# An MLP cut into eight equal chunks of seven products, an early modulation, a fourth place for weights, and smaller edits to mask and router bias

## The chip, the cores and the metric

The kernel runs on one core of a Trainium2 chip. The metric is the time of one execution on the device in microseconds (us); lower is better. The engines are TensorE (PE, matrix products), VectorE (DVE), ScalarE (ACT), GpSimd (POOL) and SyncE (SP, which issues nearly all transfers). Each engine runs its instructions in the order in which they were written to it.

## The reference

Two transformer blocks over 1024 rows of 1024 float32 numbers, one after the other. What the change touches:

```python
# first block: causal conv + retention mixer, cross attention to 256 memory rows, then
h = h + square(relu(rmsnorm(h, norm_mlp_w) @ up_w)) @ down_w      # up 1024x4096, down 4096x1024
x = rmsnorm(h, norm_f_w)
# second block
mod   = silu(c)     @ w_ada + b_ada                               # w_ada 1024x6144, six vectors of 1024
mod_c = silu(c_ctx) @ w_ada + b_ada                               # only its first two vectors are used
h = rmsnorm(x, g_mix) * (1 + sc1) + sh1
# q, k, v and a short convolution from h @ w_in; rope; 8 query heads on 2 key heads
# softmax over [sink, 256 context keys, latent keys with |i - j| <= 128]
x = x + gt1 * (concat(att, conv) @ w_out)
h2 = rmsnorm(x, g_ffn) * (1 + sc2) + sh2
# router: softmax(h2 @ w_router); each of 16 experts takes its 128 best rows; silu gate, up, down
x = x + gt2 * experts(h2);  return rmsnorm(x, g_final)
```

## The kernel before, in words

Every large product is made of float32r matmuls on split numbers: a number is a rounded part and a remainder, and a product is three matmuls (hi·hi, hi·lo, lo·hi; `mm3`). A matrix of weights arrives as a raw unit of 128x1024 float32 (`raw_unit`, 512 KB, issued by SP) and is split by ACT (a copy, L119) and DVE (a subtraction, L120) into a place `w`.

The program goes through its stages in this order: conv and retention; the mixer's output product (`add_out` on `w_out_tm`, tile `wo`); cross attention; the MLP; the second block's norm with keys and values (`kv`), queries, attention, output product, router, top rows, experts. A scheduler merges the stages' instructions on each engine from the order of the code and the priorities (`tc.high_priority`); what it decides is fixed when the kernel is built.

The MLP holds the normalised input of 512 rows as eight tiles for each half of the rows (`hm[0]`, `hm[1]`), and the sum of 1024 rows as eight tiles `acc`. It walks over nine chunks of the hidden dimension (in blocks of 128, `fb`): two chunks of two blocks, and seven of four. The first two and the last chunk are standard (`mlp_chunk`): "up" of each block and half, then "dn" by output tile, three matmuls for each block. The last is ordered by row tile, so that tile 0 of `acc` is complete first. The six between (`mlp_chunk_7`) replace the eight block products of a 2x2 block matrix product by seven, with sums and differences of blocks made on DVE: seven products of 24 matmuls (tiles `dnA`, `dnB`, `dnC`). The "up" results are squared into T places 4 to 7 as full numbers, and split into the operands `x..`/`s..`.

The modulation (`mod_blocks`) multiplies each of 48 units of `w_ada` (through the one place R32) with the rows `crow` (silu of c and c_ctx, T places 4 to 7) in reductions on DVE (L767): four for each of the first 16 units, two for the others. The table `MOD_BLOCKS` says after which chunk of the MLP how many units stand.

After the MLP each of the eight row tiles is normalised twice (L955 to L973; `z` is L972), with many one-column instructions (L169 to L180, L966 to L970) on DVE. Four `z` tiles are transposed (`ptT`), scaled on ACT (L234) and split on DVE (L235, L236) into `hT`, which the products `kv` read; `kT` (L1018) is the first transpose of a finished key tile.

PSUM banks go round in rings: `pm = Ring([0, 1, 2, 3, 4])` for products, `pt = Ring([5, 6, 7])` for transposes (`ptT`), `pu = Ring([4, 5, 6, 7])` for the "up" tiles of `mlp_chunk_7`. The input tiles `hin` from which `hm[1]` is made lie in R17 to R20, and `mlp_chunk_7` puts its first operands into R16 to R19.

Of the kernel before, what the change touches and what calls it, by code (L numbers as in the profile page):

```python
# [10 lines left out]
F32 = mybir.dt.float32  # L11
F32R = mybir.dt.float32r
# [8 lines left out]
MLP_CHUNKS = [2, 2] + [4] * 7  # L21
MOD_BLOCKS = [8, 8] + [5] * 6 + [2]
# [13 lines left out]
def tile_kernel(ctx: ExitStack, tc: tile.TileContext, d, out, stop=None, dbg=None):  # L36
# [93 lines left out]

    def wunits(src, i0, n, ahead=1500):

        res = []
        with tc.high_priority(offset=ahead):
            for u in range(i0, i0 + n):
                raw = raw_unit(src[u])
                w = sb.tile([128, 2, 1024], F32R, tag=f"W{w_ring[0]()}", bufs=1, name=nm("w"))
                split(w[:, 0, :], w[:, 1, :], raw)
                res.append(w)
        return res  # L140
# [531 lines left out]
    add_out(x_d, d["w_out_tm"], mT, range(8), h1_d, "h1", lambda: R(hxR(), [128, 512], name="hx"))  # L672
    hq[0] = normed(h1_d, 0, g_x, [19, 20, 21, 16], H[0], "hq")
# [75 lines left out]

    mod_d = dram([4, 1024], "mod_d")  # L750
    mws = T(8, [128, 512], name="mws")
    mjunk = mws[:, 0:256].bitcast(BF)
    mpart = mws[:, 256:384].rearrange("p (h n) -> p h n", h=2)
    crow = {}
    for o in range(2):
        for h in range(2):
            c = bcast(T(4 + 2 * o + h, [128, 512], name="crow"), d["c_rows"][o, h * 512:(h + 1) * 512], 512)
            act.activation(c, c, AF.Silu)
            crow[o, h] = c

    def mod_blocks(b0, n):

        for b in range(b0, b0 + n):
            raw = load(R(32, [128, 1024], name="wada"), d["w_ada"][b])
            for o in range(2 if b < 16 else 1):
                for h in range(2):
                    dve.tensor_tensor_reduce(out=mjunk, in0=raw[:, h * 512:(h + 1) * 512], in1=crow[o, h],  # L767
                                             op0=OP.mult, op1=OP.add, scale=1.0, scalar=0.0,
                                             accum_out=mpart[:, h, 48 * o + b:48 * o + b + 1])

    rr = Ring([0, 1])
    rv = Ring([2, 3])
    UT = {0: [16, 21, 22, 23], 1: [17, 18, 19, 20]}

    def mlp_chunk(ch, ch0, fbs, last):

        uT = {0: [], 1: []}
        for fb in range(fbs):
            uni = wunits(d["up_fm"], ch0 + fb, 1)
            for half in range(2):  # L780
                p = B(pm(), "up")
                fm_block(p, uni[0], half_of(hm, half))
                r = T(rr(), [128, 512], name="relu")
                act.activation(r, p, AF.Relu)
                v = T(rv(), [128, 512], name="sq")
                act.activation(v, r, AF.Square)
                ut = R(UT[half][fb], [128, 2, 512], F32R, name="uT")
                dve.tensor_copy(ut[:, 0, :], v)
                dve.tensor_sub(ut[:, 1, :], v, ut[:, 0, :].bitcast(F32))
                uT[half].append(ut)  # L790
        nu = fbs // 2
        if not last:
            order = [(nb, t) for nb in range(2) for t in range(8)]
        else:
            order = [(nb, t) for t in range(8) for nb in range(2)]
        uni = {}
        for nb, t in order:
            if nb not in uni:
                uni[nb] = wunits(d["down_tm"], ch0 + nb * nu, nu)
            sl = slice(nb * 512, (nb + 1) * 512)  # L800
            p = B(pm(), "dn")
# [756 lines left out]
```

## Time and profile before

| | |
|---|---|
| median of three runs | 2522.18 us (2521.58 to 2522.71) |
| the profiled execution's own time | 2525.16 us |
| its span in the trace | 2523.2 us (1.96 us less than its time) |
| PE busy over the span | 2400.3 us, 95% |
| DVE busy | 1898.4 us, 75% |
| ACT busy | 1240.8 us, 49% |
| mean granted clock of PE | 0.98 |

A share over the whole span says little here, since PE is the limit in most stages and waits in a few: the stages have to be read one by one. The busy time of pipelined matmuls overlaps; their spacing is what counts.

### The profile page before, as it was taken

What the parts mean: (1) busy time and instruction counts of PE and PEld (TensorE: products, weight loads), DVE (VectorE), ACT (ScalarE), POOL (GpSimd) and SP (SyncE); (2) the same over time, 40 slices, a digit from 0 to 9 for tenths busy, and PEclk for the clock granted to TensorE, in tenths of its full rate; (3) what the DMA queues carried; (4) which work ended last, traced back from release to release, by engine and by line L of the source; (5) the groups of instructions that cost most, each with busy time, mean ns of one, the idle gap of its engine ahead of it and who ended that gap; (6) DMA issues with size and microseconds to landing.
All of it is one profiled execution on the core that took longest, in us unless ns stands there. A gap on an engine that the chain in (4) does not pass through costs nothing. (4 is left out here: it accounts for less than half of the span.)

```text
span 2523.2 us, 31350 instructions
## 1 busy us (share of the span) xinstructions
PE 2400.3 (95%) x11327; PEld 1947.9 (77%) x11327; DVE 1898.4 (75%) x3269; ACT 1240.8 (49%) x1891; POOL 56.5 (2%) x37
## 2 busy tenths in 40 slices
PE   7999899999999999999999899999985999999995
PEld 6887677888878788888888777777873888888774
DVE  6999893554566877775566758776658999999887
ACT  6113552454451342334335725554334888887775
POOL 0000000000000000000000000000000110101100
PEclk9999999999999999999999999999996999999998
DMA  4233555425353244421222121114674999999994
GB/s 179 100 127 112 175 163 180 155 77 179 116 180 101 92 134 143 143 79 42 67 84 78 70 83 51 38 55 155 235 262 154 388 399 394 393 394 391 355 372 158
DMA packets 139051, 444.88 MB, mean 176 GB/s; under 512 B 15728, under 2 KB 20240, under 8 KB 138896
## 3 DMA queue, kind: packets, MB, share of 16 engines
q1 hardware_dynamic: 134144, 425.58, 47.6%
q0 software_dynamic: 4752, 17.30, 2.7%
q8 instruction: 89, 1.46, 0.2%
q14 instruction: 66, 0.54, 0.1%
HBM read 390.37 MB, written 52.45 MB: 176 GB/s over the span
## 5 line engine op out<-in xcount | busy, mean ns | idle before, releaser
L119 ACT ACTIVATE w<-raw 128x1024 fp32r<-128x1024 f32 x576 | 601.4, 1059 | 608.6 <-PE up L146 107.5
L120 DVE TENSOR_TENSOR w<-raw,w 128x1024 fp32r<-128x1024 f32 x576 | 692.6, 1223 | 164.8 <-ACT w L119 153.3
L144 PE MATMUL up<-hm,w 128*128 128x512 f32 x512 | 199.6, 390 | 0.0
L145 PE MATMUL up<-hm,w 128*128 128x512 f32 x512 | 199.4, 389 | 0.0
L146 PE MATMUL up<-hm,w 128*128 128x512 f32 x512 | 199.3, 389 | 0.0
L424 DVE SCALAR_TENSOR_TENSOR y<-u,small,y 128x1023 f32<-128x1023 f32 (+25 forms) x120 | 146.2, 1267 | 0.4
L767 DVE CUSTOM_DVE_ANT_0 mws<-wada,crow 128x512 bf16<-128x512 f32 x128 | 88.1, 688 | 49.0 <-DMA wada<-w_ada 47.3
L144 PEld LDWEIGHTS up<-hm,w 128*128 128x128 f32 x512 | 96.0, 188 | 20.3 <-DVE acc L846 0.3
L145 PEld LDWEIGHTS up<-hm,w 128*128 128x128 f32 x512 | 96.1, 188 | 19.8
L146 PEld LDWEIGHTS up<-hm,w 128*128 128x128 f32 x512 | 96.1, 188 | 19.8
L145 PE MATMUL dn<-w,x1T 128*128 128x512 f32 x256 | 101.5, 396 | 2.0 <-DVE w L120 2.0
L145 PE MATMUL ga<-w,x1T 128*128 128x512 f32 x256 | 101.7, 397 | 1.7 <-DVE w L120 1.7
L144 PE MATMUL dn<-w,x1T 128*128 128x512 f32 x256 | 102.3, 400 | 0.5 <-ACT w L119 0.5
L146 PE MATMUL ga<-w,x1T 128*128 128x512 f32 x256 | 101.2, 396 | 0.0
L146 PE MATMUL dn<-w,x1T 128*128 128x512 f32 x256 | 101.2, 395 | 0.0
L145 PE MATMUL up<-w,x1T 128*128 128x512 f32 x256 | 100.8, 394 | 0.2 <-DVE w L120 0.2
L144 PE MATMUL ga<-w,x1T 128*128 128x512 f32 x256 | 100.7, 393 | 0.0
L146 PE MATMUL up<-w,x1T 128*128 128x512 f32 x256 | 99.8, 390 | 0.0
L144 PE MATMUL up<-w,x1T 128*128 128x512 f32 x256 | 99.8, 390 | 0.0
L839 PE MATMUL dnB<-w,s 128*128 128x512 f32 x288 | 71.3, 403 | 5.8 <-ACT s L119 4.1
L846 DVE TENSOR_TENSOR acc<-dnA,acc 128x512 f32<-128x512 f32 x96 | 63.2, 686 | 11.4 <-PE dnA L839 10.9
L1353 POOL DMA_INDIRECT xs<-hf_d,IT x16 | 19.8, 1237 | 2264.9 <-DVE IT L1340 1925.6
(460 smaller groups left out, 5814.4 us busy)
## 6 DMA issues: line engine op xcount, KB each, us to landing
raw<-experts SPq DMA_DIRECT2D x384, 512.0 KB, 7.2
wada<-w_ada SPq DMA_DIRECT2D x48, 512.0 KB, 3.6
raw<-down_tm SPq DMA_DIRECT2D x38, 512.0 KB, 3.6
raw<-up_fm SPq DMA_DIRECT2D x32, 512.0 KB, 3.6
raw<-w_out_tm SPq DMA_DIRECT2D x24, 512.0 KB, 4.1
raw<-w_in_fm SPq DMA_DIRECT2D x20, 512.0 KB, 4.0
h_d<-hx SPq DMA_DIRECT2D x32, 256.0 KB, 2.9
raw<-xq_fm SPq DMA_DIRECT2D x16, 512.0 KB, 4.9
```

What stands on the lines that cost most here:

```text
L119: act.activation(hi, src, AF.Copy)
L120: dve.tensor_sub(lo, src, hi.bitcast(F32))
L144: pe.matmul(out_, l[0], r[0], start=first, stop=False)
L145: pe.matmul(out_, l[0], r[1], start=False, stop=False)
L146: pe.matmul(out_, l[1], r[0], start=False, stop=last)
L424: dve.scalar_tensor_tensor(yc[:, s:], uc[:, :1024 - s], convw[:, c, 30 - s:31 - s], yc[:, s:], op0=OP.mult, op1=OP.add)
L767: dve.tensor_tensor_reduce(out=mjunk, in0=raw[:, h * 512:(h + 1) * 512], in1=crow[o, h], op0=OP.mult, op1=OP.add, scale=1.0, scalar=0.0, a ...
L839: pe.matmul(bank[j], l, r, start=first and f + i == 0, stop=f == 1 and i == 2, skip_group_check=not first)
L846: dve.tensor_add(a[:, sl], bank[j], a[:, sl])
L1353: nc.gpsimd.indirect_dma_start(out=xs, out_offset=None, in_=hf_d, in_offset=bass.IndirectOffsetOnAxis(ap=IT[:, e:e + 1], axis=0))
```

## The change

The MLP has eight chunks of four blocks, all of seven products. The first takes the "up" tiles in another order (`first`), and the last its seven products in another order (`end`). A pair of registers R34 and R35 is a fourth place for split weights and R33 a fourth for raw units in the MLP; later R33 to R35 hold raw units of the experts. Room for them comes from a DMA scratch of 4096. The modulation is 64 blocks of two reductions with one pair of `crow` (T4, T5), so that 16 units are loaded twice. Of these blocks 28 stand right after the first `add_out`, with three places, the others in the MLP's chunks with one place. In attention the mask is added to the two outer blocks of 128 keys only, after the first part of the scores. The router's bias product `lb` is made right after the modulation. The diff, cut:

```diff
-MLP_CHUNKS = [2, 2] + [4] * 7
-MOD_BLOCKS = [8, 8] + [5] * 6 + [2]
+MLP_CHUNKS = 8
+MOD_EARLY = 28
+MOD_BLOCKS = [2, 6, 6, 6, 6, 6, 4, 0]
...
+    class Pair:
+        def __init__(self, i):
+            self.t = [R(i + j, [128, 1024], F32R, name="w") for j in range(2)]
+        def __getitem__(self, ix):
+            _, j, sl = ix
+            return self.t[j][:, sl]
+    def w_place():
+        i = w_ring[0]()
+        if i == "pair":
+            return Pair(34)
+        return sb.tile([128, 2, 1024], F32R, tag=f"W{i}", bufs=1, name=nm("w"))
...
     add_out(x_d, d["w_out_tm"], mT, range(8), h1_d, "h1", lambda: R(hxR(), [128, 512], name="hx"))
+    crow = []
+    wada = Ring([22, 23, 32])
+    def mod_blocks(b0, n):
+        for b in range(b0, b0 + n):
+            o, i = divmod(b, 48)
+            if i == 0 or b == MOD_EARLY:
+                crow[:] = [bcast(T(4 + h, [128, 512], name="crow"), d["c_rows"][o, h * 512:(h + 1) * 512], 512)
+                           for h in range(2)]
+                for c in crow:
+                    act.activation(c, c, AF.Silu)
+            raw = load(R(wada(), [128, 1024], name="wada"), d["w_ada"][i])
+            for h in range(2):
+                dve.tensor_tensor_reduce(out=mjunk, in0=raw[:, h * 512:(h + 1) * 512], in1=crow[h],
+                                         op0=OP.mult, op1=OP.add, scale=1.0, scalar=0.0,
+                                         accum_out=mpart[:, h, b:b + 1])
+    mod_blocks(0, MOD_EARLY)
+    wada = Ring([32])
...
-    def mlp_chunk_7(ch0):
+    def mlp_chunk(ch0, first, end):
...
-        for f in range(2):
+        for f, half in ((0, 0), (1, 0), (0, 1), (1, 1)) if first else ((0, 0), (0, 1), (1, 0), (1, 1)):
...
+        else:
+            ...
+            product(bB, xD, t1, True)
+            add(bB, 1, 1)
+            product(bA, xE, t2, False)
+            add(bA, 0, 1)
+            ...
+            product(bB, xG, w22, False)
+            add(bB, 0, 1)
+            bC = [B(4 + j, "dnC") for j in range(4)]
+            product(bC, xF, w21, True)
+            add(bC, 0, 0)
+            product(bA, xB, t3, False)
+            add(bA, 1, 1)
+            product(bA, xC, t4, False)
+            add(bA, 1, 0)
...
+    w_ring[0] = Ring([0, 1, 2, "pair"])
+    raw_ring[0] = Ring([("raw", 0), ("raw", 1), ("raw", 2), ("R", 33)])
+    mb = MOD_EARLY
+    for ch in range(MLP_CHUNKS):
+        mlp_chunk(4 * ch, ch == 0, ch == MLP_CHUNKS - 1)
...
-                    pe.matmul(pl, identr, wmr[:, m0:m0 + nl], start=True, stop=False)
-                    for l in range(2):
-                        pe.matmul(pl, qT[:, h, :], K2[2 * kv + l][:, lo * 128:lo * 128 + nl],
-                                  start=False, stop=(l == 1))
+                    pe.matmul(pl, qT[:, h, :], K2[2 * kv][:, lo * 128:lo * 128 + nl], start=True, stop=False)
+                    if nl == 384:
+                        pe.matmul(pl.rearrange("p (b n) -> p b n", b=3)[:, 0:3:2, :], identr,
+                                  wmr[:, 0:256].rearrange("p (b n) -> p b n", b=2), start=False, stop=False)
+                    else:
+                        o = 0 if t > 0 else 128
+                        pe.matmul(pl[:, o:o + 128], identr, wmr[:, o:o + 128], start=False, stop=False)
+                    pe.matmul(pl, qT[:, h, :], K2[2 * kv + 1][:, lo * 128:lo * 128 + nl], start=False, stop=True)
...
-                       + [("raw", i) for i in range(3)] + [("R", i) for i in H[1] + [32]])
+                       + [("raw", i) for i in range(3)] + [("R", i) for i in H[1] + [32, 33, 34, 35]])
...
-    nc = bacc.Bacc("TRN2", target_bir_lowering=False, num_devices=1)
+    nc = bacc.Bacc("TRN2", target_bir_lowering=False, num_devices=1, dynamic_dma_scratch_size=4096)
```

Where the MLP begins, PE before has the transposes of the first `hin` tile (row tile 4 of the second half), then "up" matmuls, and the transposes of the next tile after 15 of them:

```order
L146 MATMUL wo_5925<-w_5833,oT_5545 128x512
L247 MATMUL ptT_6020<-ident,hin_5952 128x128
L247 MATMUL ptT_6028<-ident,hin_5952 128x128
L247 MATMUL ptT_6036<-ident,hin_5952 128x128
L144 MATMUL up_6119<-hm_5621,w_6116 128x512
L145 MATMUL up_6119<-hm_5621,w_6116 128x512
```

PE in the changed kernel at the same place:

```order
L164 MATMUL wo_6045<-w_5953,oT_5665 128x512
L265 MATMUL ptT_6140<-ident,hin_6072 128x128
L265 MATMUL ptT_6148<-ident,hin_6072 128x128
L265 MATMUL ptT_6156<-ident,hin_6072 128x128
L265 MATMUL ptT_6140<-ident,hin_6089 128x128
L265 MATMUL ptT_6148<-ident,hin_6089 128x128
L265 MATMUL ptT_6156<-ident,hin_6089 128x128
L162 MATMUL up_6229<-hm_5741,w_6226 128x512
L163 MATMUL up_6229<-hm_5741,w_6226 128x512
```

The transposes of the second tile now stand ahead of every "up" matmul. Up to the last transpose of the fourth tile (32 transposes in all) there are 24 matmuls of `up_6229`, 3 of `up_6407` and 5 of `dnA`; the next 24 matmuls of the first half (`up_6264`) come behind it. Before, 76 matmuls of "up" and "dn" stand in that stretch.

DVE where the MLP ends, in the changed kernel: `acc_6204` to `acc_6210` are the row tiles of the first half, `acc_6212` to `acc_6218` those of the second; `dnC` completes the first half, `dnA_10282` to `dnA_10285` are the banks of the last product, and L191 is the reciprocal in the norm of row tile 0:

```order
L831 TENSOR_TENSOR acc_6204<-dnC_10590,acc_6204 128x512
...
L831 TENSOR_TENSOR acc_6212<-dnA_10282,acc_6212 128x512
L831 TENSOR_TENSOR acc_6214<-dnA_10283,acc_6214 128x512
L831 TENSOR_TENSOR acc_6216<-dnA_10284,acc_6216 128x512
L831 TENSOR_TENSOR acc_6218<-dnA_10285,acc_6218 128x512
L191 RECIPROCAL y_10719<-y_10717 128x1
L187 TENSOR_SCALAR y_10753<-y_10748 128x1
L979 TENSOR_TENSOR acc_6208<-acc_6208,bc_10678 128x1024
```

Before, five of the eight `z` stand ahead of DVE's last addition of a "dn" tile, and 73 instructions stand between that addition and the first instruction on a finished `kv` tile (L986). Now no `z` stands ahead of it, and 163 instructions stand between: 83 more of one column, five more `z`, four more products with the norm's gain (L962 before, L979 now), and two splits of weights fewer.

DVE ahead of the first `wo` product's operands in the changed kernel; `mT` are the operands, L710 the reductions of the modulation:

```order
L619 TENSOR_SCALAR z_2772<-yc_2751,y_2757,y_2770 128x512
L710 ISA mws_3797<-wada_3816,crow_3798 128x512
L710 ISA mws_3797 128x1
L710 ISA mws_3797<-wada_3816,crow_3800 128x512
...
L710 ISA mws_3797<-wada_3824,crow_3800 128x512
L710 ISA mws_3797 128x1
L122 TENSOR_TENSOR mT_2781<-zsl_2779,mT_2781 128x512
L122 TENSOR_TENSOR mT_2791<-zsl_2789,mT_2791 128x512
L710 ISA mws_3797<-wada_3828,crow_3798 128x512
```

Before, the splits of `mT` (L120) stand right behind the `z` (L601). Up to the last of the operands the reductions of about eleven blocks are now between them, and on SP seven loads of `w_ada` stand ahead of the loads of `yr`, from which half of the operands are made.

## Rows read from the trace of the kernel before

**Rows 1.** The page's first part: busy time, share of the span, instructions.
```profile
PE 2400.3 (95%) x11327; PEld 1947.9 (77%) x11327; DVE 1898.4 (75%) x3269; ACT 1240.8 (49%) x1891; POOL 56.5 (2%) x37
```

**Rows 2.** Windows: length, PE, PEld, DVE, ACT, POOL busy (instructions), clock, DMA share, GB/s.
```profile
363.40:396.00 32.60, 31.04 (x160) 23.77 (x161) 23.27 (x58) 18.57 (x30) 0.00 (x0) 1.00 0.51 168
396.00:461.00 65.00, 65.00 (x288) 53.83 (x288) 21.68 (x47) 13.07 (x19) 0.00 (x0) 1.00 0.59 190
705.80:733.40 27.60, 23.88 (x117) 18.22 (x115) 19.80 (x46) 20.24 (x31) 0.00 (x0) 1.00 0.56 194
...
850.00:900.00 50.00, 44.18 (x177) 34.50 (x176) 42.56 (x74) 18.16 (x27) 0.00 (x0) 0.93 0.41 127
...
1351.80:1389.80 38.00, 38.00 (x170) 31.40 (x169) 31.84 (x111) 24.87 (x47) 0.00 (x0) 1.00 0.18 70
1389.80:1411.30 21.50, 17.36 (x131) 15.18 (x128) 21.28 (x82) 17.24 (x33) 0.00 (x0) 1.00 0.42 148
...
2000.00:2300.00 300.00, 300.00 (x1384) 246.34 (x1384) 287.99 (x277) 244.29 (x260) 28.59 (x17) 1.00 1.03 394
```

**Rows 3.** Timeline of PE in a seven-product chunk: start, us, what, count.
```profile
1242.58 5.60 PE L839 MATMUL dnA<-w,x 128*128 128x512 f32 x24
1248.02 0.39 PE L144 MATMUL up<-hm,w 128*128 128x512 f32 x1
```

**Rows 4.** Timeline, first seven-product chunk; in brackets idle time ahead and its end.
```profile
849.27 0.69 DVE L767 CUSTOM_DVE_ANT_0 mws<-wada,crow 128x512 bf16<-128x512 f32 x1 [2.51 <-DMA wada<-w_ada]
...
851.48 0.60 ACT L821 ACTIVATE sq<-up 128x512 f32<-128x512 f32 x1 [10.27 <-DVE mws L767]
...
854.31 3.85 PE L839 MATMUL dnB<-w,s 128*128 128x512 f32 x9 [3.62 <-ACT s L119]
858.00 2.89 PE L839 MATMUL dnA<-w,s 128*128 128x512 f32 x12
```

**Rows 5.** The attention's mask line by form.
```profile
L1104 PE MATMUL s<-wmr x64: 277/354/448, 1500.2 to 1731.6; 128*128 128x384 f32 x48, 128*128 128x256 f32 x16
```

**Rows 6.** Timeline of PE at the router's bias.
```profile
1768.54 1.93 PE L1203 MATMUL lb<-wr,modT 128*128 128x16 f32 x16 [0.83 <-issue]
```

**Rows 7.** Timeline of PE and DVE at the MLP's start.
```profile
725.46 0.49 PE L247 MATMUL ptT<-ident,hin 128*128 128x128 f32 x3
...
732.68 0.75 DVE L230 SCALAR_TENSOR_TENSOR hm<-ptT,small,hm 128x512 fp32r<-128x512 f32 x1
```

**Rows 8.** Timeline of DVE and PE at the MLP's end.
```profile
1351.77 0.69 DVE L803 TENSOR_TENSOR acc<-dn,acc 128x512 f32<-128x512 f32 x1 [1.44 <-PE dn L146]
...
1362.12 0.75 DVE L972 TENSOR_SCALAR z<-acc,y 128x1024 f32<-128x1024 f32 x1
...
1389.42 0.39 PE L146 MATMUL dn<-w,uT 128*128 128x512 f32 x1
...
1411.30 0.90 PE L1018 MATMUL kT<-ident,kd 128*128 128x128 f32 x4 [1.64 <-ACT kd L1014]
```

**Rows 9.** Timeline of DVE in the norm behind the MLP: short and long instructions.
```profile
1358.20 0.16 DVE L177 TENSOR_TENSOR y<-y,y 128x1 f32<-128x1 f32 x1
1358.39 0.15 DVE L178 TENSOR_SCALAR y<-y 128x1 f32<-128x1 f32 x1
...
1396.26 0.15 DVE L177 TENSOR_TENSOR y<-y,y 128x1 f32<-128x1 f32 x1
1396.33 1.22 DVE L962 TENSOR_TENSOR acc<-acc,bc 128x1024 f32<-128x1024 f32 x1
1397.47 0.15 DVE L970 TENSOR_TENSOR y<-y,y 128x1 f32<-128x1 f32 x1
```

**Rows 10.** Timeline of DVE ahead of the first output product.
```profile
380.71 1.29 DVE L120 TENSOR_TENSOR mT<-zsl,mT 128x512 fp32r<-128x512 f32 x2 [2.42 <-ACT mT L119]
...
393.77 1.42 DVE L230 SCALAR_TENSOR_TENSOR mT<-ptT,small,mT 128x512 fp32r<-128x512 f32 x2 [1.01 <-ACT mT L229]
```

**Rows 11.** The page's transfers: issues, KB each, us to landing.
```profile
wada<-w_ada SPq DMA_DIRECT2D x48, 512.0 KB, 3.6
```

More of the change, by code (lines that the diff above doesn't have):

```diff
@@ L136, in wunits @@
                 raw = raw_unit(src[u])
[L137 removed]
+                w = w_place()
                 split(w[:, 0, :], w[:, 1, :], raw)
@@ L747, in tile_kernel @@
     acc = [load(R(24 + t, [128, 1024], name="acc"), h2_d[rows(t), :]) for t in range(8)]
[L750 to L801, printed above, removed]
-            tm_block(p, tile_of(uT, t), uni[nb])
-            dve.tensor_add(acc[t][:, sl], p, acc[t][:, sl])
@@ L894, in mlp_chunk_7 @@
-        add(bA, 0, 1)
-        with tc.high_priority(offset=1500):
-            y21 = raw_unit(d["down_tm"][ch0 + 1])
-            dve.tensor_sub(y11, y21, y11)
-            t4 = wsplit(y11)
-            w22 = wsplit(y22)
-            w21 = wsplit(y21)
-        product(bA, xB, t3, False)
-        add(bA, 1, 1)
-        product(bA, xC, t4, False)
-        add(bA, 1, 0)
-        product(bB, xG, w22, False)
-        add(bB, 0, 1)
-        bC = [B(j, "dnC") for j in range(4)]
-        product(bC, xF, w21, True)
@@ L925, in tile_kernel @@
         mb += n
+    w_ring[0] = Ring(range(5))
+    raw_ring[0] = Ring([("raw", i) for i in range(3)])
     def row_bc(i, r):
@@ L953, in tile_kernel @@
     store(mod_d.rearrange("r (k p) -> (r k) p", k=8), mrow)
+    wr0 = load(T(7, [128, 8, 16], name="wr0"), d["w_router"].rearrange("p (k e) -> p k e", k=8))
+    p = B(pt(), "lb")
+    for k in range(8):
+        pe.matmul(p[:, :16], sh2c[:, k:k + 1].to_broadcast([128, 128]), wr0[:, k, :], start=(k == 0), stop=(k == 7))
+    lbias = cst.tile([128, 16], F32, name="lbias")
+    act.activation(lbias, p[:, :16], AF.Copy)
     x2_d = dram([1024, 1024], "x2_d")
@@ L1090, in attention @@
         nl = (hi - lo + 1) * 128
-        m0 = 0 if t > 0 else 128
         for kv in range(2):
@@ L1199, in tile_kernel @@
     load(wr, d["w_router"].rearrange("p (k e) -> p k e", k=8))
-    p = B(7, "lb")
-    for k in range(8):
-        pe.matmul(p[:, :16], sh2c[:, k:k + 1].to_broadcast([128, 128]), wr[:, k, :], start=(k == 0), stop=(k == 7))
-    lbias = cst.tile([128, 16], F32, name="lbias")
-    act.activation(lbias, p[:, :16], AF.Copy)
     dve.tensor_mul(wr, wr, a2c[:, :, None].to_broadcast([128, 8, 16]))
@@ L1516, in layout @@
     dn = f["mlp_down_w"]
-    chunks, r0 = [], 0
-    for fbs in MLP_CHUNKS:
-        chunks.append(_tm(dn[r0:r0 + fbs * 128], [0, 512]))
-        r0 += fbs * 128
+    chunks = []
+    for ch in range(MLP_CHUNKS):
+        chunks.append(_tm(dn[ch * 512:(ch + 1) * 512], [0, 512]))
     a["down_tm"] = np.concatenate(chunks, 0)
```

94 lines of the change are left out of this document (57 added, 37 removed).

## The prediction, made before the changed kernel ran

> **What bounds the kernel now.** I read the busy shares first: PE has 95% of the span [rows 1], so time can only go where PE issues fewer matmuls or stops waiting, and comes back wherever PE is made to wait. Then the windows, to see in which stages PE has no spare time [rows 2]: it is fully busy from 396 to 461, to the end of the MLP at 1389.8 and from 2000 to 2300. It waits a little ahead of the output product (31.04 of 32.60), at the MLP's start (23.88 of 27.60) and behind the MLP (17.36 of 21.50), where DVE is busy for 21.28 of 21.50. The reader is to see that the MLP's last stretch is full on both: from 1351.8 to 1389.8 DVE works 31.84 of 38.00 under PE's matmuls. Then the timelines, for what one matmul costs: 24 matmuls of 128x512 start at 1242.58 and the next at 1248.02 [rows 3], 5.44/24 = 0.2267 us each (their busy time overlaps and is not used).
>
> **The change, part by part.** Gains first.
>
> *Seven products.* A standard chunk of four blocks has 8 x 2 x 12 = 192 "dn" matmuls, one of seven products 7 x 24 = 168. The two small chunks and the last make two such chunks, so 48 matmuls go: 48 x 0.2267 = **-10.9**. PE is fully busy in the MLP's inside, so all of it counts there.
>
> *The stall near 850.* In the first seven-product chunk ACT waits 10.27 us for a T place on which DVE still reads `crow`; DVE itself waits 2.51 us for `wada` [rows 4]. PE then waits 3.62, and its next 9 matmuls need 858.00 - 854.31 = 3.69 us, 0.41 each, where 0.2267 is usual: 3.62 + 9 x 0.18 = 5.3 lost here alone. From 850 to 900 PE made 177 matmuls [rows 2], where 50/0.2267 = 220.6 have room: 43.6 x 0.2267 = 9.9 us lost in all (the busy time hides part of it, since slow matmuls count as busy). With one pair of `crow` in T4 and T5, places 6 and 7 are free: **-9.9** (5.3 at least).
>
> *Mask.* 64 mask matmuls have 384 or 256 columns [rows 5] and 128 fewer afterwards. 128 columns of a 512-column matmul take 0.2267/4 = 0.057 us: 3.6, of which I take **-3.3** (nothing to 3.6).
>
> *Router bias.* 16 matmuls are busy for 1.93 us with 0.83 idle ahead [rows 6], and most of them go to where PE waits anyway, ahead of the first `z`, the others into the last product: **-2.2** (nothing to 2.8).
>
> *Places for the experts.* Three more raw units are 1.57 MB, at 394 GB/s [rows 2] 4.0 us of lead for a stage where transfers and PE are both full: nothing to 4.0. Transfers are already ahead for most of it: **-1**.
>
> These make -27.3. Now what comes back.
>
> *The MLP's start.* `hm[1]` must be transposed and split before the second half can start; its last tile arrives at 725.46, and the last split starts at 732.68 [rows 7]. Between its first and last transpose PE had 76 matmuls, and has 32 now (the second tile's transposes stand ahead of all "up" work; and the "up" ring of banks 4 to 7 shares three banks with the transposes' ring of 5 to 7, and operands share R17 to R19 with `hin`, so little else can run). 44 x 0.2267 = 10.0 of cover gone. Of the raw loads that stand between the last `hx` stores and the last `hin` load on SP, fewer do so now, so the tile may come somewhat earlier, which I put at 2 us, an estimate between nothing and the 5.4 of two matmul groups: **+8** (5 to 10).
>
> *Early modulation.* 28 blocks are 56 reductions of 0.69 [rows 4], 39 us of DVE. From 396 on DVE has 43 us free under full PE [rows 2], but about eleven blocks, 22 reductions or 15 us, stand ahead of the last operands. DVE is idle for 32.6 - 23.3 = 9.3 us there. Its splits of `mT` begin at 380.71 and its last operands are at 393.77 [rows 10]; 15 - 9.3 = 5.7 of lateness at least if they only fill idle time; with the idle time lying elsewhere, up to 9; and less where PE has earlier work. The queue of SP matters too: seven loads stand ahead of those of `yr`, and only three have a place at once. **+5** (nothing to 9). What is queued behind a late reduction is `mT` itself, and PE waits for that. In the MLP 56 reductions fewer lie on DVE, worth nothing, since PE hides them.
>
> *The MLP's end.* Before, tile 0 of `acc` is complete at 1351.77 + 0.69, 37 us ahead of the last "dn" matmul, and the first `kT` follows that matmul by 1411.30 - 1389.42 = 21.9 us [rows 8], in which DVE is 99% busy [rows 2]. Now the first half is complete 10.9 us ahead of PE's end (two products of 24 matmuls). But on DVE its norm's reciprocal stands behind the addition of the last product's last bank, so the norm of row tile 0 cannot go on before PE's end, however early its sums are. From there to the first `kv` there were 73 instructions, now 163: 83 more of one column, five `z`, four products with the gain, two splits fewer. One-column instructions follow each other by 0.07 (two alternating, 1396.26 to 1396.33) to 0.19 (dependent), the product with the gain takes 1.14 (1396.33 to 1397.47) [rows 9], a `z` 0.75 at most [rows 8], a split as much as the gain. So 5.8 to 15.8, +3.8, +4.6, -2.3: 11.9 to 21.9. Most come in pairs of two tiles, and ACT has its squares and copies of the same tiles (17.24 of 21.50 busy already), so I take the middle: **+17**.
>
> The sum is -27.3 + 8 + 5 + 17 = +2.7. Against the profiled execution's 2525.16 us (1.96 around its span) this is 2527.9; that execution lies 3.0 above the median of the runs shown, so in their terms 2522.2 + 2.7 = 2524.9, rounded to **2525**. About 0.2% (5 us) is what a measurement of this kernel can tell from no change: below 2517 is faster, above 2527 slower.
>
> A rule bears on the last term. The Trainium skill says in "TensorE: Matmul & The Clock Gate", section "Architectural detail", that VectorE and ScalarE are strict first-in, first-out queues. No row here shows an instruction of DVE overtaking another. By that rule the early half gains nothing on DVE while the additions stand ahead; without it the sum would be that of the first rival.
>
> **The rivals.** *A: the end is cheap.* If the norm of the first half runs under the last two products, some two more tiles are left behind PE's end than before; tiles went by at (1389.4 - 1351.8)/7 = 5.4 us, less the waits for "dn" in it, so +6 instead of +17: 2514. For it: ten free microseconds of PE cover; against: the order on DVE. It decides once the end costs less than about 10.
>
> *B: the early modulation holds up the output product, slower.* Place: 363 to 396. A `wada` load lands in 3.6 us [rows 11]; of the seven loads ahead of `yr` four wait for a reduction to give up a place. If each is then waited for, 4 x 3.6 = 14.4 stands where I put 5: +9.4, 2534. It decides when over some 8 us are lost there. Against it: DMA is only half busy (0.51), so three places may keep up.
>
> *C: the change doesn't do what it says.* The stall at 850 is not gone but comes again in chunk 0, whose operands wait for `hin`'s places: +10.2, 2535. For it: the same start is short of work; against: `crow` is off T6 and T7.
>
> *D: all low.* The end at its lower 12, the start at 5, the wait for operands nothing, the experts at 4: 5 + 3 + 5 + 3 = 16 less, 2509.
>
> **How the numbers follow.** The forecast (2525, with 2517 to 2533 for itself) 0.48; A 0.22; B 0.15; C 0.08; D 0.07. The range of 8 in 10 goes from 2509 to 2539, with B and C a little exceeded and D at its lower bound. Of the forecast's 0.48, 0.03 lies below 2517, 0.27 within, 0.18 above. Faster: 0.03 + 0.20 of A + 0.07 = 0.30; same: 0.27 + 0.02 = 0.29; slower: 0.18 + 0.15 + 0.08 = 0.41.
>
> **What would show it.** 1344 rows of `dnA`, `dnB` and `dnC`, none of `dn`; no wait of ACT for `mws` in the MLP; PE waiting some 14 us in all for `hin` and `hm` at the MLP's start; `mT` operands complete about 5 us later against the stage's beginning; the first `kT` about 39 us behind the last matmul of `dnA`, with DVE nearly full in between; mask matmuls of 256 columns, and no `lb` ahead of the second output product. The prediction is wrong if `z` of tile 0 starts before the last `dnA` ends, if the stall returns in chunk 0, or if SP shows `yr` loads held behind `wada`.

## The result and the profile after

The changed kernel takes 2544.7 us (median of 4 runs, 2543.0 to 2546.3), the kernel before, run beside it, 2522.4: ratio 1.0084, 95% interval 1.0072 to 1.0096. It is slower by 0.84%, 21 us; the forecast of 2525 and its range up to 2539 were both too low.

The first part of the page after answers to [rows 1]: 48 matmuls fewer, and more work on DVE and ACT.

```profile
span 2543.1 us, 31358 instructions
PE 2394.1 (94%) x11279; PEld 1948.0 (77%) x11279; DVE 1930.1 (76%) x3303; ACT 1272.5 (50%) x1931; POOL 54.7 (2%) x37
```

Where the time went is read from the starts of the first and last matmul of each stage, in one profiled execution of each kernel (worked out from the timelines of PE; the figures are us). The rows below the difference are experiments and are used further down.

| kernel | first output product (`wo`) | cross attention to its last `wo` | MLP to last `dn` | to first `kT` | first query to second `wo` | second `wo` |
|---|---|---|---|---|---|---|
| before | 98.6 | 243.3 | 684.1 | 21.9 | 275.7 | 107.1 |
| after | 106.4 | 252.5 | 668.5 | 39.6 | 278.4 | 108.7 |
| difference | +7.8 | +9.2 | -15.6 | +17.7 | +2.7 | +1.6 |
| e1 no early modulation | 98.6 | 243.4 | 670.8 | 38.8 | 279.0 | 107.4 |
| e7 early reductions, three loads | 107.0 | 247.1 | 671.1 | 39.5 | 279.3 | 107.5 |
| e15 early loads, no reductions | 103.6 | 247.8 | 671.9 | 39.6 | 279.8 | 107.2 |
| e17 no early Silu | 107.7 | 255.1 | 671.7 | 39.6 | 280.2 | 107.6 |
| e18 early loads, no Silu | 104.0 | 250.5 | 671.2 | 38.8 | 278.6 | 108.7 |
| e8 early loads from GpSimd | 126.5 | 248.9 | 670.5 | 38.8 | 279.6 | 107.7 |
| e6 no early, standard last chunk | 98.6 | 241.8 | 675.4 | 23.9 | 279.7 | 108.7 |
| e14 e6 with the old mask | 98.5 | 242.5 | 676.6 | 23.7 | 273.3 | 107.4 |
| e9 before, mask alone | 98.8 | 242.9 | 686.4 | 21.9 | 281.4 | 108.4 |
| e13 before, mask order alone | 98.0 | 242.4 | 684.2 | 22.1 | 280.4 | 108.6 |

The other stages differ by -3.5 in all, and the sum is the +19.9 between the spans. One execution is not exact: kernels with the same order of instructions up to the MLP (the changed one, e2, e3, e4) take 106.4 to 108.1 in the first column and 247.3 to 252.7 in the second, and those without early blocks 98.0 to 98.8 and 241.6 to 243.5. So the losses there are clear, and their size in the second is known to some 5 us. The windows of the changed kernel answer to [rows 2]:

```profile
363.00:396.00 33.00, 27.04 (x124) 21.08 (x122) 29.80 (x88) 19.13 (x29) 0.00 (x0) 0.84 0.80 266
396.00:461.00 65.00, 64.68 (x294) 53.48 (x292) 41.97 (x99) 6.87 (x8) 0.00 (x0) 1.00 0.85 286
461.00:490.00 29.00, 23.23 (x100) 18.45 (x99) 18.40 (x44) 15.74 (x26) 0.00 (x0) 0.82 0.91 308
700.00:728.00 28.00, 23.03 (x103) 18.59 (x101) 12.15 (x26) 10.77 (x14) 0.00 (x0) 0.96 0.80 253
1351.90:1389.90 38.00, 38.00 (x172) 31.44 (x170) 30.97 (x43) 20.38 (x30) 0.00 (x0) 1.00 0.42 126
1389.90:1429.50 39.60, 22.97 (x143) 20.63 (x141) 35.62 (x172) 30.91 (x65) 0.00 (x0) 0.73 0.38 145
```

From 396 to 461 PE is as full as before, but the DMA share rose from 0.59 to 0.85 and DVE from 21.68 to 41.97. What is late shows behind it: from 461 to 490 PE makes 100 matmuls, where it made 154 before (461.1 to 490.1). Behind the MLP PE is busy for 23 of 39.6 us, at a granted clock of 0.73, and DVE for 35.6.

**First output product.** PE and then DVE, timelines; the brackets give the idle time ahead and its end. The DVE rows answer to [rows 10].

```profile
381.70 4.00 PE L625 MATMUL ptz<-ident,z 128*128 128x128 f32 x16 [5.29 <-DVE z L619]
...
387.20 0.80 PE L164 MATMUL wo<-w,mT 128*128 128x512 f32 x1 [0.65 <-DVE mT L122]
387.80 0.63 PE L162 MATMUL wo<-w,mT 128*128 128x512 f32 x1
388.23 0.63 PE L163 MATMUL wo<-w,mT 128*128 128x512 f32 x1
```

```profile
375.82 0.69 DVE L710 CUSTOM_DVE_ANT_0 mws<-wada,crow 128x512 bf16<-128x512 f32 x1 [0.51 <-ACT crow L707]
...
380.74 1.53 DVE L619 TENSOR_SCALAR z<-yc,y,y 128x512 f32<-128x512 f32 x2
...
386.46 1.29 DVE L122 TENSOR_TENSOR mT<-zsl,mT 128x512 fp32r<-128x512 f32 x2
...
390.31 0.69 DVE L710 CUSTOM_DVE_ANT_0 mws<-wada,crow 128x512 bf16<-128x512 f32 x1 [1.21 <-DMA wada<-w_ada]
...
401.27 1.40 DVE L248 SCALAR_TENSOR_TENSOR mT<-ptT,small,mT 128x512 fp32r<-128x512 f32 x2
```

The last two operands start 401.27 - 362.45 = 38.8 us behind the stage's first matmul; before it was 393.77 - 363.40 = 30.4 [rows 2, 10]. PE waits 5.29 for `z`, and behind that wait its matmuls are 0.43 apart (387.80 to 388.23) where 0.2267 is usual [rows 3]: the granted clock of the window is 0.84, a mix of full speed (2.4 GHz) and half (1.2 GHz).

What is new on DVE ahead of the `z` and the first split of `mT` is reductions, five from 375.82 on and six behind the `z`. None of the eleven waits for a load; the first waits 0.51 for `crow`, and a later one 1.21 for its load (390.31). On SP seven loads of `w_ada` do stand between the loads of `yr`:

```profile
376.85 12.60 SPq L344 DMA_DIRECT2D wada<-w_ada  x7
391.64 1.75 SPq L344 DMA_DIRECT2D yr<-yr  x4
```

The last `yr` leaves 30.5 us behind the stage's first matmul, where it was 22.1 before. But e7 (below) has no load of `w_ada` among the eight (SP's queue), and there it leaves at 31.2, so these loads aren't what holds it:

```profile
378.11 19.12 SPq L344 DMA_DIRECT2D yr<-yr  x8
```

**Cross attention.** SP's queue in the changed kernel, from 449 to 463, then PE where the products of `hq` begin:

```profile
449.44 5.35 SPq L344 DMA_DIRECT2D wada<-w_ada  x2
...
456.71 0.43 SPq L344 DMA_DIRECT2D hin<-h_d  x1
...
459.39 1.06 SPq L344 DMA_DIRECT2D hin<-h_d  x1
```

```profile
471.80 0.33 PE L265 MATMUL ptT<-ident,hin 128*128 128x128 f32 x1 [2.36 <-DVE hin L212]
472.66 0.33 PE L265 MATMUL ptT<-ident,hin 128*128 128x128 f32 x1 [0.53 <-DVE hin L212]
474.29 2.18 PE L265 MATMUL ptT<-ident,hin 128*128 128x128 f32 x9 [1.31 <-DVE hin L212]
...
478.89 0.80 PE L162 MATMUL q<-hq,w 128*128 128x512 f32 x1 [1.56 <-DVE hx L671]
```

The first `hin` load of this norm leaves SP at 456.71. In the kernel before, SP's queue has it at 430.83, and the others at 437, 442 and 448:

```profile
430.83 0.42 SPq L326 DMA_DIRECT2D hin<-h_d  x1
```

DVE's additions `hx`, whose stores `hin` reads, stand behind reductions that now do wait for their loads: eight such waits from 407 to 459 make 13.0 us, the longest 3.97.

```profile
453.00 0.69 DVE L710 CUSTOM_DVE_ANT_0 mws<-wada,crow 128x512 bf16<-128x512 f32 x1 [3.97 <-DMA wada<-w_ada]
```

PE waits 5.76 us in the four places shown, and from 471 to 480 its granted clock is 0.62. The MLP's start and end are shown with their experiments.

### The profile page after: what moved, and what is told of

Same layout as the page of the kernel before. It is cut to its first block, busy times and chain, and to the rows that moved or that the text cites. A ratio compares the mean times of both kernels' runs of the same rounds, so it can differ in the third digit from the quotient of the medians.

```text
span 2543.1 us, 31358 instructions
## 1 busy us (share of the span) xinstructions
PE 2394.1 (94%) x11279; PEld 1948.0 (77%) x11279; DVE 1930.1 (76%) x3303; ACT 1272.5 (50%) x1931; POOL 54.7 (2%) x37
## 5 line engine op out<-in xcount | busy, mean ns | idle before, releaser
L121 ACT ACTIVATE w<-raw 128x1024 fp32r<-128x1024 f32 x582 | 609.9, 1059 | 608.1 <-PE dnA L824 104.0
L122 DVE TENSOR_TENSOR w<-raw,w 128x1024 fp32r<-128x1024 f32 x582 | 701.2, 1223 | 163.1 <-ACT w L121 152.2
L710 DVE CUSTOM_DVE_ANT_0 mws<-wada,crow 128x512 bf16<-128x512 f32 x128 | 88.3, 690 | 48.5 <-DMA wada<-w_ada 42.2
L163 PEld LDWEIGHTS up<-hm,w 128*128 128x128 f32 x512 | 96.5, 188 | 19.9
L831 DVE TENSOR_TENSOR acc<-dnA,acc 128x512 f32<-128x512 f32 x128 | 83.9, 686 | 17.3 <-PE dnA L824 17.2
L824 PE MATMUL dnA<-w,x 128*128 128x512 f32 x384 | 90.9, 390 | 0.0
L824 PE MATMUL dnB<-w,s 128*128 128x512 f32 x384 | 89.6, 389 | 0.0
```

The source lines that it names most:

```text
L121: act.activation(hi, src, AF.Copy)
L122: dve.tensor_sub(lo, src, hi.bitcast(F32))
L163: pe.matmul(out_, l[0], r[1], start=False, stop=False)
L824: pe.matmul(bank[j], l, r, start=first and f + i == 0, stop=f == 1 and i == 2, skip_group_check=not first)
L831: dve.tensor_add(a[:, sl], bank[j], a[:, sl])
```

## The experiments

All ratios are against the kernel before, run beside it on the same chip; the edits are to the changed kernel where nothing else is said.

### The early modulation

**e1.** All 64 blocks stand in the MLP.

```diff
-MOD_EARLY = 28
-MOD_BLOCKS = [2, 6, 6, 6, 6, 6, 4, 0]
+MOD_EARLY = 0
+MOD_BLOCKS = [6, 10, 10, 10, 10, 10, 8, 0]
```

> The changed kernel with no modulation ahead of the MLP (all 64 blocks in the MLP's chunks: 6, 10, 10, 10, 10, 10, 8, 0). Theory: the early blocks cost some 16 us in all, 8 ahead of and in the first output product and 8 behind it, where the first half's input tiles for cross attention come late because SP and DVE stand waiting for w_ada loads. Then the time falls by 14 to 17, to about 2529, the last matmul of that product ends at 462 again, and no wait for hin above 1 us follows it. Rival: the late tiles have another cause (places or the smaller scratch): then it falls by at most 8, to 2537 or more. A second rival: 10 blocks a chunk through one place make DVE wait in the MLP, and PE with it: new PE waits of several us in the chunks.

2526.9 us, 1.0006 (0.9997 to 1.0016). From 1.0084 this gives back 0.0078 x 2523 = 19.7 us. The table shows where: 7.8 in `wo` and 9.1 in the cross attention. The MLP, with all reductions in it, takes 670.8, no more than in e7, e15 and e17 (671.1 to 671.9), which have 28 blocks fewer there. The term was put at 5.

**e7** keeps all reductions but only three of the early loads (25 are left out, so the reductions use other numbers); **e8** has GpSimd issue the early loads.

```diff
-            raw = load(R(wada(), [128, 1024], name="wada"), d["w_ada"][i])
+            if b < 3 or b >= MOD_EARLY:            # e7
+                raw = load(R(wada(), [128, 1024], name="wada"), d["w_ada"][i])
...
+            raw = R(wada(), [128, 1024], name="wada")        # e8
+            (nc.gpsimd if b < MOD_EARLY else nc.sync).dma_start(raw, d["w_ada"][i])
```

> The changed kernel, where the 28 early blocks load only three units of w_ada and reduce the third again and again: 25 loads left out, all reductions kept (blocks 3 to 27 give other numbers). Theory: the transfers and their place on SP's queue hold the first output product up; then the wo stage ends some 8 to 16 us earlier than in the changed kernel and the time falls by 10 to 16, to 2530 to 2535. Rival: the 56 reductions on DVE alone do it, by their place ahead of mT and hx; then it falls by less than 5.

> The changed kernel with the 28 early loads of w_ada issued by GpSimd in place of SP; nothing left out. Theory: on SP's one queue the loads of yr, hx and hin stand behind loads of w_ada that wait for a place; with their own queue the time falls by 6 to 12, to 2533 to 2539. Rival: DVE itself waits in its order for the units (up to 4 us each), with the additions hx behind; then it falls by less than 4, or rises where these transfers take longer to issue.

e7: 2540.6, 1.0056 (1.0041 to 1.0071). e8: 2564.9, 1.0164 (1.0149 to 1.0180). Reductions without loads hold up the first output product as much (107.0), the cross attention by 3.7 only (its first `hin` load leaves 79.8 us behind the first `wo` matmul, 67.5 before, 94.3 in the changed kernel). From GpSimd's queue the 28 early loads take a median of 5.6 us to land; from SP's queue the same 28 take 5.0, and the 36 later ones 3.6, so most of the difference comes with the place and not with the queue. In e8 a reduction ahead of `z` waits 4.15 us for its load (DVE), and `z` keeps PE waiting for 9.81:

```profile
386.20 0.69 DVE L711 CUSTOM_DVE_ANT_0 mws<-wada,crow 128x512 bf16<-128x512 f32 x1 [4.15 <-DMA wada<-w_ada]
```

```profile
388.90 4.00 PE L625 MATMUL ptz<-ident,z 128*128 128x128 f32 x16 [9.81 <-DVE z L619]
```

**e15** keeps the early loads and replaces the reductions by one copy of two columns for each block (28 blocks are not summed). **e17** leaves out the Silu of the early `crow` (other numbers are summed), **e18** leaves it out of e15 too.

```diff
+            if b < MOD_EARLY:                                # e15, e18
+                dve.tensor_copy(mpart[:, :, b], raw[:, 0:2])
+                continue
...
-                    act.activation(c, c, AF.Silu)
+                    if b:                                    # e17, e18
+                        act.activation(c, c, AF.Silu)
```

> The changed kernel with its 28 early loads of w_ada where they are, but a copy of two columns in place of each block's two reductions (other numbers). Theory, after the run with three loads: the reductions hold up the first output product (stage 98.6 us without, 106.4 with them), and the loads the tiles behind it; then that stage takes 99 to 101, the cross attention stage 246 to 250 where 243 is undisturbed, and the time is 2532 to 2538. Rival: loads cost nothing by themselves, and both stages are as without early blocks: 2527.

> The changed kernel with the Silu of the first pair of c rows left out (so the early 28 blocks are summed with other numbers); loads and reductions stay. Theory: in the first output product the modulation costs 7.8 us, of which about half is ACT, which must wait for the c rows' transfer (2.5 us) and load the table of Silu and that of the square root again (1.28 each) ahead of the root that every z needs; the other half is the loads and the reductions. Then the stage from the first to the last matmul of the first output product goes from 106.4 to 101 to 103 us, and the time falls by 3 to 5 us against the changed kernel's 1.0084: ratio 1.0065 to 1.0072. Rival: the operands of the product are late on DVE alone, behind reductions: the stage stays at 106 and the ratio at 1.008.

> Early loads and one copy of two columns for each in place of the reductions, and the Silu left out too (28 blocks are not summed). Theory: the loads alone do not hold up the first output product, ACT's table loads and its wait do: the stage goes from 103.6 (with Silu) to 98.6 to 100. The cross attention stays at about 247, as its first rows wait for loads behind the early ones, against 243 without. Ratio 1.003 to 1.004. Rival: the loads hold up the operands of the product on SP's queue: the stage stays at 103 or more.

e15: 2538.7, 1.0056 (1.0041 to 1.0072). e17: 2548.3, 1.0096 (1.0079 to 1.0113). e18: 2541.9, 1.0073 (1.0054 to 1.0092). Loads alone and reductions alone each cost both stages something, and the two don't add up (8.4 and 5.0 in `wo`, 7.8 together). In e15 the first `hin` leaves at 85.1. The theory of the Silu falls: without it `wo` takes 107.7 and 104.0, no less than with it. Its rival stands, DVE's order. DVE, then PE in e17:

```profile
382.90 0.69 DVE L711 CUSTOM_DVE_ANT_0 mws<-wada,crow 128x512 bf16<-128x512 f32 x1 [2.00 <-DMA wada<-w_ada]
...
386.46 1.29 DVE L122 TENSOR_TENSOR mT<-zsl,mT 128x512 fp32r<-128x512 f32 x2
```

```profile
379.96 0.52 PE L625 MATMUL ptz<-ident,z 128*128 128x128 f32 x3 [2.92 <-DVE y L196]
...
387.20 0.52 PE L164 MATMUL wo<-w,mT 128*128 128x512 f32 x1 [2.44 <-DVE mT L122]
```

A reduction waits 2.00 us for its load, and four more go by before the split of `mT`, for which PE waits 2.44. In e18, where a copy takes 0.17, DVE still waits 1.57 ahead of `z` and 2.33 ahead of `mT`:

```profile
379.65 0.17 DVE L711 COPY mws<-wada 128x2 f32<-128x2 f32 x1 [1.57 <-DMA wada<-w_ada]
379.73 1.52 DVE L619 TENSOR_SCALAR z<-yc,y,y 128x512 f32<-128x512 f32 x2
...
383.58 0.17 DVE L711 COPY mws<-wada 128x2 f32<-128x2 f32 x1 [2.33 <-DMA wada<-w_ada]
```

### The MLP's end

**e2** gives the last chunk the standard form by row tile, 24 matmuls more (24 x 0.2267 = 5.4 us); **e3** lifts the norm of the first half; **e5** and **e6** are e3 and e2 without early modulation.

```diff
+        if ch == MLP_CHUNKS - 1:                             # e2, e6
+            w_ring[0] = Ring(range(5))
+            std_chunk(4 * ch, 4)
...
+    with tc.high_priority(offset=400):                       # e3, e5
+        for t in range(4):
+            norm_tile(t)
...
+    with tc.high_priority(offset=400):
+        hT2[0] = to_fm(zs[:4], H[0], pt, name="hT2", gain=a1, shift=sh1)
```

> The changed kernel with the last chunk standard and ordered by row tile, as in the kernel before: 24 matmuls more (+5.4 us), and five of the eight z ahead of DVE's last addition again. Theory: the MLP's end costs 17.7 us by the order on DVE; then the first kT comes 22 us behind the last dn matmul instead of 40, and the time falls by 17.7 - 5.4 = 12, to 2532. Rival: something else than the last chunk's order holds the norm up (the bias product, the weights' places): then the time rises by up to 5, to 2550.

> The changed kernel with seven products in the last chunk as it is, but with the norm of the first half's four row tiles and their transposes and splits given priority, so that on DVE 77 instead of 163 instructions stand between the last addition and the first instruction on a kv tile. Theory (the order on DVE decides, not the moment at which the sums are complete): the first kT comes some 22 to 26 us behind the last product, and the time falls by 12 to 17, to about 2530. Rival (the amount of work behind the MLP decides: the second half's norm then holds up its own keys instead): it falls by less than 5.

> No early modulation, and the norm of the first half with priority: the two edits that by the profiles undo the two large losses, with seven products kept in all chunks. Theory (the losses are independent of each other): the time of the run without early blocks less the 8 to 10 us that the end gives back, 2517 to 2520 where the kernel before takes 2524.7, so faster by 0.2 to 0.3%. Rival (they share their cause, a late start that the end would have hidden): 2525 or more.

> No early modulation, and the last chunk standard and ordered by row tile. Theory: 24 matmuls more than with seven products, but the norm runs under them; 2516 to 2519, within 3 us of the variant with the norm of the first half first. Rival (the order by row tile was worth little and the gain came from the first half's early norm alone): 2524 or more.

e2: 2530.6, 1.0023 (1.0013 to 1.0032). e3: 2540.1, 1.0064 (1.0047 to 1.0081). e5: 2523.4, 0.9996 (0.9987 to 1.0005). e6: 2514.1, 0.9961 (0.9947 to 0.9974). DVE in the changed kernel, then PE (they answer to [rows 8]):

```profile
1390.34 0.69 DVE L831 TENSOR_TENSOR acc<-dnA,acc 128x512 f32<-128x512 f32 x1 [0.18 <-PE dnA L824]
1390.94 0.15 DVE L191 RECIPROCAL y<-y 128x1 f32<-128x1 f32 x1
...
1395.12 1.41 DVE L989 TENSOR_SCALAR z<-acc,y 128x1024 f32<-128x1024 f32 x2
```

```profile
1395.92 1.56 PE L265 MATMUL ptT<-ident,z 128*128 128x128 f32 x6 [4.38 <-DVE z L989]
1400.28 0.90 PE L265 MATMUL ptT<-ident,z 128*128 128x128 f32 x3 [2.79 <-DVE z L989]
1405.28 0.90 PE L265 MATMUL ptT<-ident,z 128*128 128x128 f32 x3 [4.10 <-DVE z L989]
```

The reciprocal of row tile 0 starts behind the last addition, and the first `z` 5.2 us behind PE's end. The Trainium skill says in "TensorE: Matmul & The Clock Gate", section "Architectural detail", that ScalarE's and VectorE's queues are strictly first-in, first-out; the order seen here agrees with it (1390.94 behind 1390.34). In e6 five `z` go by before the last addition of a "dn" tile (DVE, timeline and window):

```profile
1371.75 0.75 DVE L1023 TENSOR_SCALAR z<-acc,y 128x1024 f32<-128x1024 f32 x1
...
1378.43 0.68 DVE L821 TENSOR_TENSOR acc<-dn,acc 128x512 f32<-128x512 f32 x1
1385.86 0.75 DVE L1023 TENSOR_SCALAR z<-acc,y 128x1024 f32<-128x1024 f32 x1
```

```profile
1379.70:1403.60 23.90, 19.03 (x128) 16.31 (x126) 22.41 (x93) 17.67 (x39) 0.00 (x0) 0.93 0.46 165
```

The way to `kT` falls from 38.8 (e1) to 23.9, and the time by 11 us from e1 to e6 (0.0045 x 2523), in spite of 24 more matmuls. Lifting the norm shortens that way too (39.6 to 31.4 in e3), but `kT`'s own stage grows by 3.1, and the time gains 3 to 5 us at most: 77 rows still lie behind the last addition. e3's profiled execution took 2529.7 us and its three others 2539.7 to 2542.1. Of the 15.1 us by which its span is below the changed kernel's, 12.3 lie in stages that the edit doesn't touch: 2.8 ahead of the first output product, 5.2 in the cross attention, 4.3 behind the second output product. The end itself gives 8.2 - 3.1 = 5.1 there, as the times do. Why those stages were shorter in that execution is open.

### Mask and router bias

The kernel before with the mask's edit alone (**e9**), with its order alone and the columns as before (**e13**), with the moved bias alone (**e10**).

```diff
-                    pe.matmul(pl, identr, wmr[:, m0:m0 + nl], start=True, stop=False)
-                    for l in range(2):
-                        pe.matmul(pl, qT[:, h, :], K2[2 * kv + l][:, lo * 128:lo * 128 + nl],
-                                  start=False, stop=(l == 1))
+                    pe.matmul(pl, qT[:, h, :], K2[2 * kv][:, lo * 128:lo * 128 + nl], start=True, stop=False)
+                    pe.matmul(pl, identr, wmr[:, m0:m0 + nl], start=False, stop=False)          # e13
+                    pe.matmul(pl, qT[:, h, :], K2[2 * kv + 1][:, lo * 128:lo * 128 + nl], start=False, stop=True)
...
+    wr0 = load(T(7, [128, 8, 16], name="wr0"), d["w_router"].rearrange("p (k e) -> p k e", k=8))    # e10
+    p = B(pt(), "lb")
...
-    p = B(7, "lb")
```

> The kernel before with the mask's part of the change alone. Theory: the products lose some 2.4 us of columns but the stretch from the first q2T to the second output product gets longer by 3 to 4 us, since the scheduler lays the filler products otherwise around the attention; so 0 to 3 us slower than before. Rival (my prediction's): 3.3 us faster.

> The kernel before with the mask product moved behind the first product with the keys, and nothing else (it keeps its 384 or 256 columns). Theory: the mask product needs no query, so that it could start a score tile while its queries were still being split; behind the keys' product it can't, and the stretch from q2T to the second output product gets longer by itself, by 5 us or more: 2530 to 2535, as with the whole mask edit. Rival: the two-block form of the mask product is what costs; then the time stays within 3 us of before.

> The kernel before with the router's bias product moved behind the modulation, alone. Theory: its 1.8 us of matmuls ahead of the second output product had covered a wait for that product's operand (m); without them PE waits 2.5 us there and runs the next matmuls at half clock, so the time stays within 1.5 us or rises by up to 2. Rival (my prediction's): 2.2 us faster.

e9: 2531.7, 1.0032 (1.0020 to 1.0044), slower by 7.2 us. e13: 2528.5, 1.0019 (1.0010 to 1.0028), slower by 5. e10: 2521.9, 0.9989 (0.9980 to 0.9998), faster by 2.6. The fewer columns are there: the mask's line in e9 answers to [rows 5], 280 ns where 354 was the median.

```profile
L1105 PE MATMUL s<-wmr x48: 274/280/364, 1527.6 to 1701.5; 128*128 128x256 f32 x48
```

But ACT's copies of the transposed probabilities, which PE's next product needs, wait longer for PE. Groups by line from the first query to the second `wo`: before, then e9.

```profile
L226 ACT ACTIVATE P2h<-P2T 128x512 fp32r<-128x512 f32 x76 | 43.0, 596 | 41.7 <-PE P2T L1132 33.0 <-PE o L1141 5.4 <-DVE PW L1126 1.6
```

```profile
L226 ACT ACTIVATE P2h<-P2T 128x512 fp32r<-128x512 f32 x76 | 42.3, 596 | 55.0 <-PE P2T L1135 53.2 <-PE o L1144 1.7
```

That the place costs, whatever the columns, e13 shows: with all columns and the mask behind the first scores the stage takes 280.4 instead of 275.7. Why it costs is open. The mask needs no queries, so ahead of the scores it could run while PE had none yet, and behind them it can't; but PE's waits for the queries `qT` are short with either order (0.3 us before, 0.1 in e13). The build also lays out the rest of the stage anew: without the mask's own rows, some 390 of PE's 1337 matmuls there stand in another order. What grows is PE's waits ahead of the short convolution's products `cg` and `bg`, from 1.7 to 5.1 us (2.6 in e9). No run moved the mask and held the rest in its place.

### The MLP's start, and the stall

**e4** takes the old order of the "up" tiles in chunk 0 (`first=False`). **e12** is the kernel before with one pair of `crow` and 64 blocks.

```diff
-        mlp_chunk(4 * ch, ch == 0, ch == MLP_CHUNKS - 1)
+        mlp_chunk(4 * ch, False, ch == MLP_CHUNKS - 1)       # e4
...
-MOD_BLOCKS = [8, 8] + [5] * 6 + [2]
+MOD_BLOCKS = [8] * 8 + [0]                                   # e12
```

> The changed kernel with the first chunk's up tiles in the usual order (half 0, half 1 of each block) instead of both blocks of half 0 first. Theory: the loss at the MLP's start (12 us of PE, 5.6 more than before) comes from the banks and places that the up tiles share with the transposes, which this order doesn't change; then the time stays within 3 us of 2545. Rival: the order of the up tiles is what leaves PE without cover: then it moves by 5 or more.

> The kernel before with 64 modulation blocks of two reductions and one pair of crow in T4 and T5 (eight blocks behind each of the first eight chunks), alone. Theory: the stall at 850 goes and nothing comes for it: 9 to 10 us faster, with no PE wait above 1 us from 750 to 1380. Rival: with 16 loads more and eight blocks a chunk through one place DVE waits for w_ada elsewhere, and half of it or more comes back: less than 5 us faster.

e4: 2542.2, 1.0069 (1.0052 to 1.0086): the new order gains nothing. e12: 2515.4, 0.9964 (0.9950 to 0.9977), 9.2 us faster. In its window PE makes 217 matmuls, 177 before [rows 2]; 40 x 0.2267 = 9.1. In the profiled execution, the slowest of its five (2520.7), the MLP is only 5.4 us shorter than before, and PE waits 1.65 for DVE at 1111, where none above 1 was expected.

```profile
850.00:900.00 50.00, 49.12 (x217) 40.33 (x216) 39.76 (x71) 14.49 (x19) 0.00 (x0) 1.00 0.49 151
```

### Put together

**e11** is e6 with the old mask and the old bias, **e14** e6 with the old mask alone. **e16** is e14 with other banks for the first four "up" tiles:

```diff
+        pq = [Ring([4, 3, 2, 1]) if first else pu]
...
-            p = B(pu(), "up")
+            p = B(pq[0](), "up")
```

> No early modulation, last chunk standard by row tile, and mask and router bias as in the kernel before. Theory: the stretch from q2T to the second output product takes 276 again instead of 279.7, so 3 to 5 us faster than the same kernel with the new mask and bias: about 2510 where before takes 2524.7. Rival: mask and bias are worth what I forecast, and the time rises by 2 to 5, to 2517.

> No early modulation, last chunk standard by row tile, mask as before, router bias moved. Theory: the bias alone gave 2.6 us and adds to the 2510.2 of the same kernel with the old bias: 2506 to 2509. Rival: the gain depends on the schedule around it, and the time stays at 2510 or above.

> The kernel with the old mask and the new bias, and PSUM banks 4, 3, 2, 1 for the first four up tiles of chunk 0 instead of 4, 5, 6, 7, of which three are the transposes'. Theory: the second up tile no longer waits for a transpose bank, so 24 matmuls (5.4 us) move under the wait for the last hin tile; the MLP stage gets shorter by 4 to 6 us and the time falls to 2502 to 2505. Rival: the places R17 to R19, which the operands share with hin, hold it up all the same: less than 1.5 us.

e11: 2510.2, 0.9948 (0.9934 to 0.9961). e14: 2507.5, 0.9938 (0.9924 to 0.9951). e16: 2500.7, 0.9912 (0.9897 to 0.9927), which beats both kernels. By the ratios the old mask gives 5.8 us (e6 to e14; 7.7 by the table's two last stages), the moved bias 2.5 (e11 to e14, inside the intervals), the banks 6.6 (e14 to e16). The MLP's start in e14, then in e16 (PE); in the changed kernel the same three waits are 3.84, 2.48 and 1.59:

```profile
707.96 0.90 PE L265 MATMUL ptT<-ident,hin 128*128 128x128 f32 x3 [4.07 <-DVE hin L212]
...
711.38 0.80 PE L162 MATMUL up<-hm,w 128*128 128x512 f32 x1 [2.52 <-ACT w L121]
...
721.84 0.49 PE L162 MATMUL up<-hm,w 128*128 128x512 f32 x1 [1.60 <-ACT hm L247]
```

```profile
704.41 0.55 PE L265 MATMUL ptT<-ident,hin 128*128 128x128 f32 x3 [1.76 <-DVE hin L212]
...
707.95 0.50 PE L162 MATMUL up<-hm,w 128*128 128x512 f32 x1 [2.54 <-ACT w L121]
```

With banks that the transposes don't use, the wait for `hin` is 1.76 instead of 4.07, that for `hm` is gone, and the MLP takes 668.8 where e14 takes 676.6.

## Why the prediction was wrong, step by step

| term | predicted | measured |
|---|---|---|
| seven products | -10.9 | 48 matmuls gone |
| stall at 850 | -9.9 | -9.2 alone (e12) |
| the MLP's start | +8 | +5.9 in the profiled pair, +6.5 to +9.3 in e1 to e4, e7 and e15 |
| early modulation | +5 | +17.0 by stages, +19.7 in time (e1) |
| the MLP's end | +17 | +17.7 |
| mask | -3.3 | +7.2 alone (e9), 5.8 back when undone (e14) |
| router bias | -2.2 | -2.6 (e10), -2.5 (e14) |
| experts' places | -1 | -1.8 in the profiled pair, -1.3 in e8, -4.6 to -6.5 in the 13 others that have them |

The start is read from the time between the last `wo` ahead of the MLP and the 200th 512-column matmul behind it: 54.3 us before, 60.2 in the changed kernel, 60.8 to 63.6 in the six others. The experts' places were not tried alone; their row is the time from the last matmul of the second `wo` to the end.

**The early modulation is the step that failed most.** Inside the stage for which I worked it out the result was within its bounds and came by the way forecast, reductions ahead of the operands: 15 us of reductions less idle time came to 5.7 to 9 us of lateness, and it was 8.4, with 7.8 lost; I took the lower end. The sign of rival B is there, `yr` loads behind `wada` on SP, but e7 shows that the product is as late without it. The wrong sentence is "From 396 on DVE has 43 us free under full PE". DVE did have it; but 28 loads and their waits stand ahead of other things in the order of SP and DVE, and so the norm behind the product got its `hin` 26 us later, and the next stage took 9.2 us more. I looked for cover for DVE's busy time, not for what is queued behind each wait. e7 and e15 show that loads and reductions each do it: `hin` comes 12 us later by the reductions, 18 by the loads, 27 by both (each counted from the first `wo` matmul), and that stage takes 3.7, 4.4 and 9.2 us more.

**The mask failed in its sign.** "Nothing to 3.6" left out a loss, although the change moves the mask from a place where it needs no queries to one behind a matmul that does. I counted columns (right, e9's line) and not what another order does to the stage. That the other order costs is shown; how it does is not.

Right: products, stall, bias and the end. The mechanism forecast for the end is the one that runs, DVE's and ACT's rows behind the last addition; e2 and e6 show its price by taking it away. The start lies within its bounds (5 to 10), and the "up" tiles' banks, named there as a reason, are one (e16). Rivals A, C and D didn't come: no cheap end, no stall in chunk 0.

With the measured sizes of the two terms that failed the sum would have been 2.7 + 12.0 + 10.5 = +25.2; the median rose by 22.3 (the span of the profiled execution by 19.9). The rest is no more than the terms vary: e1 has 19.7 for the first and e14 5.8 for the second, and behind the second `wo` most executions gave more than was forecast.

## What to carry to other kernels

When work is moved under a full engine, ask of every load and every wait what stands behind it in the same queue, up to the end of the next stage; free busy time on the engine that runs it is not enough, and the moved work's own length counts wherever an operand stands behind it. A product with fewer matmuls can lose at its end if the next stage's chain needs finished rows early: e6 made 24 more matmuls and was 11 us faster than e1. And an operation that gets cheaper but changes its place in the order is a new schedule: e13 lost 5 us with the columns unchanged. Try the place apart from the columns.

## What the runs showed of the hardware that was not expected

A 512 KB load from SP's queue took a median of 5.0 us to land among the 28 early ones (DMA share 0.80 and 0.85 in their two windows) and 3.6 among the 36 later ones (share 0.46 from 731 to 950); from GpSimd's queue the 28 early ones took 5.6 (e8). A wait can cost PE more than its length: behind the 5.29 us for `z` the granted clock was 0.50 (1.2 GHz) from 381.0 to 391.2, and the matmuls started 0.43 us apart instead of 0.2267. Not every wait does: at the MLP's start before, PE waited 2.35 us for `hin`, and the clock of that window stayed at 1.00 [rows 2].
